# Weight sums of the block products tied to their place in the VectorE order

## The chip, the cores and the metric

The kernel runs on one core of a Trainium2 chip. The metric is the device time in microseconds (us) of one execution of the whole program. Engines are named as the profile names them: PE is TensorE (matmuls), PEld its weight loads, DVE is VectorE, ACT is ScalarE, POOL is GpSimd and SP is SyncE, which here issues nearly all DMAs. Each engine works through its instructions in one fixed order and waits at the head of that order for whatever the next instruction needs.

## The reference

A decoder trunk of two layers on x of 512 tokens by 1024 features. A layer is a half-step SwiGLU feed-forward, a gated token mixing of three attention branches, and a second half-step SwiGLU. The change touches only the two feed-forwards of each layer:

```python
def _swiglu(t, w_gate, w_up, w_down):
    return (jax.nn.silu(t @ w_gate) * (t @ w_up)) @ w_down

for l in range(L):
    f = _swiglu(_rmsnorm(h, ffn1_pre_g[l]), ffn1_w_gate[l], ffn1_w_up[l], ffn1_w_down[l])
    h = h + 0.5 * _rmsnorm(f, ffn1_post_g[l])
    ...   # mixing: stick-breaking, forgetting and memory attention, gated and merged
    f = _swiglu(_rmsnorm(h, ffn2_pre_g[l]), ffn2_w_gate[l], ffn2_w_up[l], ffn2_w_down[l])
    h = h + 0.5 * _rmsnorm(f, ffn2_post_g[l])
```

D_MODEL is 1024 and D_FF is 2816, that is 22 tiles of 128 hidden rows. Everything is float32.

## The kernel before

**Precision.** Every float32 operand of a matmul is split into a high part in a shorter format and a low part that holds the rest. ScalarE makes the high part of a weight tile (line 182, `wh`), and VectorE then the low part from the raw tile and the high one (line 183, `wl`). TensorE does three matmuls for each product (lines 205 to 207): high by high, high by low, low by high.

**The four feed-forwards.** They are called a and c: 0a and 0c in layer 0, 1a and 1c in layer 1 (the letter stands in each name; the order rows below cut the layer's number). Of the 22 hidden tiles the first sixteen, two chunks of eight (ci = 0 and 1), are computed with seven block products in place of eight, as in Strassen's and Winograd's schemes; the remaining six tiles (16 to 21) are plain matmuls ("plain pairs"), and are put between the block products. For each chunk there is a gate group and an up group of seven products (`token_products`, called token-major since the tokens stand on the output's partitions), in this text G0, U0, G1 and U1. Then comes one down group for both chunks (`products`), in which the two chunks take turns.

**A weight unit.** A product n (0, 2, 1, 3, 4, 5, 6 in this order) consists of two units, k = 0 and k = 2, each of two weight tiles of 128 x 512. The unit `gc_1_2_0` is the gate of feed-forward c, chunk 1, product 2, k = 0; `da_1_1_0` is of the down group of a, chunk 1, product 1. `fetch` brings a unit's raw block by one DMA of 512 KB (line 297, on the SP queue, when a slot of the ring `raw` or `o` has come free). For n = 2, 3, 5 and 6, `load` first makes a **weight sum** on VectorE (line 327): a difference of the raw block and a kept block (`tg`, `tu` or `bt`), which takes the place of one of the two. Then ScalarE casts (line 182), and VectorE makes the low part (line 183). High and low parts live in rings of four buffers, so a unit can be split only when TensorE is done with the unit four places back. TensorE works twelve matmuls on a unit. `BlockUnit` (line 270 on) holds all this. There are 192 weight sums in the program: 128 in the token-major groups and 64 in the down groups.

**What else is on VectorE and ScalarE in these groups.** In the gate and up groups: sums of the activations (lines 700 to 725, tiles x00, x11 and others, with their splits `uh` and `ul`), evictions of the products from PSUM (lines 775 to 786), and `turn`, which transposes a finished block of hidden activations: ScalarE copies it apart (line 800, tiles `th`), SP issues a DMA that transposes (line 801, `tr`), and ScalarE copies the result back into the hidden rows `hr` (line 804). In the down group: the first factors (lines 838 to 846, tiles `as`) and their splits `ah` and `al`.

**What sets the order.** Units are loaded ahead of their use by a queue object `Q`, in Python's order of tracing. The tile framework's scheduler then sets the order of each engine and may move an instruction ahead of others that it doesn't depend on. `tc.keep_in_program_order(ins)` adds an edge without a semaphore: `ins` stays behind the instruction that was traced last before it on the same engine. In the kernel before, a weight sum gets that edge only while `Q.pinned` is set, which is a short stretch outside these groups.

## Time and profile before

| what | us |
| --- | --- |
| median of three runs | 2383.31 |
| lowest and highest run | 2377.81 and 2385.16 |
| the profiled execution | 2377.93 |
| its span in the profile | 2376.2 |
| TensorE busy in the span | 2347.3 |
| VectorE busy | 1800.1 |
| ScalarE busy | 1511.8 |

The granted clock of TensorE is 0.996 of full speed over the span. The profiled execution is one near the fast end of the three runs. A row of the timeline gives the start, the length, the engine, line and operation with output and inputs, and in brackets the idle time of that engine just before and what ended it. Rows of the profile cut the numbers of a unit (`wl_dc` for all down units of c); which unit a row is follows from its place in the order.

### The profile page before, as it was taken

How to read it: one execution, taken by the hardware profiler on the slowest of the kernel's cores; microseconds unless marked ns; L12 is line 12 of the kernel's file. 1: busy time of each engine (PE TensorE's matmuls, PEld its weight loads, DVE VectorE, ACT ScalarE, POOL GpSimd, SP SyncE). 2: the span in 40 equal slices, each digit the busy share in tenths (PEclk: the TensorE clock that was granted, in tenths of full speed). 3: DMA queues.
4: the chain of work that ended last, by engine and by line, in shares of the span. 5: the costliest groups of instructions: out<-in, count | busy, mean ns of one | idle time of the engine just before them, and what ended most of it. 6: DMA issues, size and time to landing. Idle time of an engine off the chain costs nothing.

```text
span 2376.2 us, 31130 instructions
## 1 busy us (share of the span) xinstructions
PE 2347.3 (99%) x11719; PEld 1986.0 (84%) x11719; DVE 1800.1 (76%) x2358; ACT 1511.8 (64%) x2305; POOL 75.4 (3%) x134
## 2 busy tenths in 40 slices
PE   9999999999999999999999999999999999999998
PEld 7787889888888888878888878899888888888787
DVE  8876877677777688868788768766767777887785
ACT  6776465576766556774556765646777665567744
POOL 0000000000111000000000000000000100000000
PEclk9999999999999999999999999999999999999999
DMA  5666454223323555664646664542323235566743
GB/s 204 185 177 199 154 190 142 80 83 88 89 74 104 192 189 160 186 186 146 226 127 198 205 171 147 194 129 72 94 76 98 72 117 188 174 185 175 214 144 142
DMA packets 299754, 354.98 MB, mean 149 GB/s; under 512 B 78266, under 2 KB 192978, under 8 KB 299604
## 3 DMA queue, kind: packets, MB, share of 16 engines
q1 hardware_dynamic: 299508, 352.97, 48.5%
q8 instruction: 92, 1.51, 0.3%
q14 instruction: 58, 0.48, 0.1%
q0 software_dynamic: 96, 0.03, 0.0%
HBM read 319.39 MB, written 16.78 MB: 141 GB/s over the span
## 4 chain that ended last, share of the span: by engine, by line
PE 89%; DMA 3%; DVE 3%; ACT 2%; issue 1%; SPq 0%; POOL 0%; DVEq 0%; ACTq 0%
PE pg L206 4%; PE pg L207 4%; PE pg L205 4%; PE pda L206 3%; PE pdc L206 3%; PE pda L207 3%; PE pda L205 3%; PE pdc L207 2%; PE pdc L205 2%; PE pb L206 2%; PE pb L207 2%; PE pb L205 2%; PE pwo L206 1%; PE pq L206 1%; PE pq L205 1%
## 5 line engine op out<-in xcount | busy, mean ns | idle before, releaser
L205 PE MATMUL pg<-us_a,wh_wg 128*128 128x512 f32 x384 | 151.0, 393 | 0.0
L206 PE MATMUL pg<-us_a,wh_wg 128*128 128x512 f32 x384 | 149.8, 390 | 0.0
L207 PE MATMUL pg<-us_a,wl_wg 128*128 128x512 f32 x384 | 149.8, 390 | 0.0
L206 PE MATMUL pda<-wl_da,aha 128*128 128x512 f32 x224 | 89.0, 398 | 6.6 <-DVE wl_da L183 6.6
L206 PE MATMUL pdc<-wl_dc,ahc 128*128 128x512 f32 x224 | 88.7, 396 | 6.1 <-DVE wl_dc L183 6.1
L183 DVE TENSOR_TENSOR wl_da<-raw_da,wh_da 128x1024 fp32r<-128x1024 f32 x50 | 60.8, 1223 | 37.4 <-ACT wh_da L182 37.3
L205 PE MATMUL pda<-wh_da,aha 128*128 128x512 f32 x224 | 88.2, 397 | 0.8 <-ACT wh_da L182 0.5
L207 PE MATMUL pda<-wh_da,ala 128*128 128x512 f32 x224 | 88.4, 395 | 0.0
L183 DVE TENSOR_TENSOR wl_dc<-raw_dc,wh_dc 128x1024 fp32r<-128x1024 f32 x50 | 60.9, 1222 | 35.8 <-ACT wh_dc L182 35.8
L207 PE MATMUL pdc<-wh_dc,alc 128*128 128x512 f32 x224 | 87.9, 393 | 0.0
L205 PE MATMUL pdc<-wh_dc,ahc 128*128 128x512 f32 x224 | 87.4, 393 | 0.4 <-ACT wh_dc L182 0.4
L207 PEld LDWEIGHTS pg<-us_a,wl_wg 128*128 128x128 f32 x384 | 72.1, 188 | 15.2
L205 PEld LDWEIGHTS pg<-us_a,wh_wg 128*128 128x128 f32 x384 | 72.1, 188 | 14.1
L206 PEld LDWEIGHTS pg<-us_a,wh_wg 128*128 128x128 f32 x384 | 72.2, 188 | 14.1
L182 ACT CAST wh_da<-raw_da 128x1024 fp32r<-128x1024 f32 x50 | 52.1, 1049 | 41.1 <-PE pda L207 11.1
L186 DVE SCALAR_TENSOR_TENSOR wl_wg<-raw_wg,wh_wg 128x1024 fp32r<-128x1024 f32 x48 | 58.4, 1221 | 23.0 <-ACT wh_wg L185 23.0
L182 ACT CAST wh_dc<-raw_dc 128x1024 fp32r<-128x1024 f32 x50 | 52.1, 1047 | 35.3 <-DMA raw_dc<-in_ffn_w_down_dram 11.5
L200 DVE SCALAR_TENSOR_TENSOR ga<-pg,bgate,ga 128x512 f32<-128x512 f32 x48 | 35.9, 747 | 48.7 <-ACT ga L199 48.7
L182 ACT CAST wh_uc<-raw_uc 128x1024 fp32r<-128x1024 f32 x44 | 46.4, 1054 | 37.6 <-PE pwc0g L207 8.6
L185 ACT ACTIVATE wh_wg<-raw_wg 128x1024 fp32r<-128x1024 f32 x48 | 50.5, 1057 | 25.5 <-PE pv L1096 11.7
L183 DVE TENSOR_TENSOR wl_uc<-raw_uc,wh_uc 128x1024 fp32r<-128x1024 f32 x44 | 53.7, 1220 | 16.7 <-ACT wh_uc L182 16.6
L182 ACT CAST wh_ua<-raw_ua 128x1024 fp32r<-128x1024 f32 x44 | 46.2, 1052 | 28.7 <-PE pga L206 7.2
(647 smaller groups left out, 8057.2 us busy)
## 6 DMA issues: line engine op xcount, KB each, us to landing
raw_da<-in_ffn_w_down_dram SPq DMA_DIRECT2D x66, 512.0 KB, 4.9
raw_dc<-in_ffn_w_down_dram SPq DMA_DIRECT2D x66, 512.0 KB, 3.8
raw_ga<-in_ffn_w_gate_dram SPq DMA_DIRECT2D x52, 512.0 KB, 4.7
raw_ua<-in_ffn_w_up_dram SPq DMA_DIRECT2D x52, 512.0 KB, 4.6
raw_gc<-in_ffn_w_gate_dram SPq DMA_DIRECT2D x52, 512.0 KB, 4.1
raw_uc<-in_ffn_w_up_dram SPq DMA_DIRECT2D x52, 512.0 KB, 4.2
raw_wg<-in_w_gate_dram SPq DMA_DIRECT2D x48, 512.0 KB, 3.5
raw_wo<-in_w_out_dram SPq DMA_DIRECT2D x24, 512.0 KB, 3.6
```

The lines of the kernel that those rows point to most:

```text
L182: both = [nc.scalar.copy(h_ap, src)]
L183: make = lambda: nc.vector.tensor_tensor(l_ap, src, h_ap.bitcast(F32), ALU.subtract)
L185: both = [nc.scalar.activation(h_ap, src, AF.Copy, scale=scale)]
L186: make = lambda: nc.vector.scalar_tensor_tensor(l_ap, src, scale, h_ap.bitcast(F32), ALU.mult, ALU.subtract)
L200: nc.vector.scalar_tensor_tensor(t, z, minus, t, ALU.max, ALU.add)
L205: nc.tensor.matmul(pt, lh, rh, start=start, stop=False, skip_group_check=free)
L206: nc.tensor.matmul(pt, lh, rl, start=False, stop=False, skip_group_check=free)
L207: nc.tensor.matmul(pt, ll, rh, start=False, stop=stop, skip_group_check=free)
```

## The change

Units get a flag `behind`, which is set for all units of the token-major and the down groups. Where it is set, the weight sum gets the edge of `keep_in_program_order`: it stays behind the VectorE instruction that was traced last before it, which is mostly the low split (line 183) of the unit loaded before. No instruction is added, and none is taken away. In the changed file lines after 816 are shifted by 2, and after 894 by 4.

```diff
--- before.py
+++ after.py
@@ -284,7 +284,7 @@
         def __init__(self, n, src, rows, k0, nk, ncol, keep, name, place="raw"):
             super().__init__(src, k0, nk, 0, ncol, name)
             self.n, self.rows, self.keep, self.fetched, self.place = n, rows, keep, False, place
-            self.heir = None
+            self.heir, self.behind = None, False
 
         def inherits(self, un):
             un.heir, self.place = self, None
@@ -325,7 +325,7 @@
                 src = raw if self.n == 5 else t
                 a, b = (t, raw) if self.n in (2, 5) else (raw, t)
                 ins = nc.vector.tensor_tensor(src, a, b, ALU.subtract)
-                if Q.pinned:
+                if Q.pinned or self.behind:
                     tc.keep_in_program_order(ins)
             self.split_from(src)
             self.loaded()
@@ -815,6 +815,8 @@
             for n in ORDER:
                 uns = [BlockUnit(n, w, ND // 2, k, 2, S, keep, f"{nm}_{n}_{k}", n in (2, 4) or next(places))
                        for k in range(0, ND // 2, 2)]
+                for un in uns:
+                    un.behind = True
                 if n in (2, 4):
                     for un, of in zip(uns, had[n - 2 + (n == 4)]):
                         un.inherits(of)
@@ -893,6 +895,8 @@
                 w = wd[l, ci * FC * P:(ci + 1) * FC * P]
                 uns = [BlockUnit(n, w, FC // 2, k, 2, S, keep[ci], f"d{name}_{ci}_{n}_{k}", ("raw", "o")[k // 2])
                        for k in range(0, FC // 2, 2)]
+                for un in uns:
+                    un.behind = True
                 if n == 4:
                     for un, of in zip(uns, had[ci, 3]):
                         un.inherits(of)
```

What moves, at three places of feed-forward 0c (the other three have the same rows there). First VectorE in the down group, where the second product starts (`dc_0_1` and `dc_1_1`), with the sums `btc_0_0` and `btc_0_2` for the units `dc_0_2_0` and `dc_0_2_2`. Before:

```order
L183 TENSOR_TENSOR wl_dc_0_1_0_9333<-raw_dc_0_1_0_9294,wh_dc_0_1_0_9332 128x1024
L838 TENSOR_TENSOR asc_0_2_9490<-hrc_0_8495,hrc_1_8454 128x1024
L183 TENSOR_TENSOR wl_dc_0_1_2_9341<-raw_dc_0_1_2_9296,wh_dc_0_1_2_9340 128x1024
L327 TENSOR_TENSOR btc_0_0_9336<-btc_0_0_9336,raw_dc_0_2_0_9338 128x1024
L327 TENSOR_TENSOR btc_0_2_9344<-btc_0_2_9344,raw_dc_0_2_2_9346 128x1024
L183 TENSOR_TENSOR wl_dc_1_1_0_9391<-raw_dc_1_1_0_9302,wh_dc_1_1_0_9390 128x1024
L183 TENSOR_TENSOR alc_0_2_9489<-asc_0_2_9490,ahc_0_2_9488 128x1024
L838 TENSOR_TENSOR asc_1_2_9560<-hrc_2_9097,hrc_3_9056 128x1024
L183 TENSOR_TENSOR wl_dc_1_1_2_9397<-raw_dc_1_1_2_9304,wh_dc_1_1_2_9396 128x1024
```

After, from the same row on:

```order
L183 TENSOR_TENSOR wl_dc_0_1_0_9333<-raw_dc_0_1_0_9294,wh_dc_0_1_0_9332 128x1024
L183 TENSOR_TENSOR wl_dc_0_1_2_9341<-raw_dc_0_1_2_9296,wh_dc_0_1_2_9340 128x1024
L183 TENSOR_TENSOR wl_dc_1_1_0_9391<-raw_dc_1_1_0_9302,wh_dc_1_1_0_9390 128x1024
L183 TENSOR_TENSOR alc_0_2_9489<-asc_0_2_9490,ahc_0_2_9488 128x1024
L840 TENSOR_TENSOR asc_1_2_9560<-hrc_2_9097,hrc_3_9056 128x1024
L183 TENSOR_TENSOR wl_dc_1_1_2_9397<-raw_dc_1_1_2_9304,wh_dc_1_1_2_9396 128x1024
L327 TENSOR_TENSOR btc_0_0_9336<-btc_0_0_9336,raw_dc_0_2_0_9338 128x1024
L842 TENSOR_TENSOR asc_0_2_9490<-asc_0_2_9490,hrc_0_8495 128x1024
L183 TENSOR_TENSOR wl_dc_0_2_0_9428<-btc_0_0_9336,wh_dc_0_2_0_9427 128x1024
L327 TENSOR_TENSOR btc_0_2_9344<-btc_0_2_9344,raw_dc_0_2_2_9346 128x1024
```

The two sums stood ahead of the splits of `dc_1_1_0` and `dc_1_1_2`. Now both stand behind them, and each stands two rows ahead of the split of its own unit.

Second, VectorE at the end of U1, where the last up units `uc_1_6_0` and `uc_1_6_2` alternate with the first down units. Here `tuc_1_0` and `tuc_1_2` are the sums for these two units, and lines 777 and 784 are evictions of products. Before (the sum `tuc_1_0` stands six rows further up):

```order
L327 TENSOR_TENSOR tuc_1_2_8825<-raw_uc_1_6_2_9105,tuc_1_2_8825 128x1024
L183 TENSOR_TENSOR wl_dc_0_0_2_9155<-raw_dc_0_0_2_8991,wh_dc_0_0_2_9154 128x1024
L784 TENSOR_TENSOR sc_1_01_8858<-hrc_3_9056,sc_1_01_8858 128x1024
L183 TENSOR_TENSOR wl_uc_1_6_0_9187<-tuc_1_0_8823,wh_uc_1_6_0_9186 128x1024
L777 TENSOR_TENSOR hrc_3_9056<-hrc_3_9056,pwc0u_0_0_8955 128x2x256
L777 TENSOR_TENSOR hrc_3_9056<-hrc_3_9056,pwc0u_0_1_8956 128x2x256
L183 TENSOR_TENSOR alc_1_0_9253<-hrc_2_9097,ahc_1_0_9252 128x1024
L183 TENSOR_TENSOR wl_uc_1_6_2_9192<-tuc_1_2_8825,wh_uc_1_6_2_9191 128x1024
```

After:

```order
L183 TENSOR_TENSOR alc_1_0_9253<-hrc_2_9097,ahc_1_0_9252 128x1024
L183 TENSOR_TENSOR wl_dc_0_0_2_9155<-raw_dc_0_0_2_8991,wh_dc_0_0_2_9154 128x1024
L784 TENSOR_TENSOR sc_1_01_8858<-hrc_3_9056,sc_1_01_8858 128x1024
L327 TENSOR_TENSOR tuc_1_0_8823<-raw_uc_1_6_0_9063,tuc_1_0_8823 128x1024
L777 TENSOR_TENSOR hrc_3_9056<-hrc_3_9056,pwc0u_0_0_8955 128x2x256
L777 TENSOR_TENSOR hrc_3_9056<-hrc_3_9056,pwc0u_0_1_8956 128x2x256
L183 TENSOR_TENSOR alc_0_1_9349<-hrc_1_8454,ahc_0_1_9348 128x1024
L183 TENSOR_TENSOR wl_uc_1_6_0_9187<-tuc_1_0_8823,wh_uc_1_6_0_9186 128x1024
L327 TENSOR_TENSOR tuc_1_2_8825<-raw_uc_1_6_2_9105,tuc_1_2_8825 128x1024
L784 TENSOR_TENSOR sc_1_11_8770<-hrc_3_9056,sc_1_11_8770 128x1024
L183 TENSOR_TENSOR wl_uc_1_6_2_9192<-tuc_1_2_8825,wh_uc_1_6_2_9191 128x1024
```

The sums have come to stand between the splits: `tuc_1_0` behind the split of `dc_0_0_2` and the eviction at line 784, `tuc_1_2` behind the split of `uc_1_6_0`. The split `alc_1_0` has moved ahead of the split of `dc_0_0_2`, and `alc_0_1` ahead of that of `uc_1_6_0`.

Third, ScalarE in G1, around the casts of `uc_0_6_2`, `gc_1_2_0` and `gc_1_2_2`, with the copies to (line 800) and from (line 804) the transposing DMAs. Before:

```order
L804 COPY hrc_0_8495<-trc0u_1_8529 128x2x4x128
L182 CAST wh_uc_0_6_2_8591<-tuc_0_2_8221 128x1024
L800 COPY thc0u_4_1_8618<-sc_0_01_8258 128x1024
L804 COPY hrc_1_8454<-trc0u_4_0_8613 128x2x4x128
L182 CAST wh_gc_1_2_0_8637<-tgc_1_0_8505 128x1024
L800 COPY thc0u_5_0_8668<-sc_0_11_8163 128x1024
L182 CAST wh_gc_1_2_2_8644<-tgc_1_2_8507 128x1024
L800 COPY thc0u_5_1_8671<-sc_0_11_8163 128x1024
L804 COPY hrc_1_8454<-trc0u_4_1_8614 128x2x4x128
```

After:

```order
L800 COPY thc0u_4_1_8618<-sc_0_01_8258 128x1024
L182 CAST wh_uc_0_6_0_8586<-tuc_0_0_8219 128x1024
L804 COPY hrc_1_8454<-trc0u_4_0_8613 128x2x4x128
L804 COPY hrc_1_8454<-trc0u_4_1_8614 128x2x4x128
L182 CAST wh_uc_0_6_2_8591<-tuc_0_2_8221 128x1024
L800 COPY thc0u_5_0_8668<-sc_0_11_8163 128x1024
L800 COPY thc0u_5_1_8671<-sc_0_11_8163 128x1024
L182 CAST wh_gc_1_2_0_8637<-tgc_1_0_8505 128x1024
L804 COPY hrc_1_8454<-trc0u_5_8666 128x2x4x128
L182 CAST wh_gc_1_2_2_8644<-tgc_1_2_8507 128x1024
```

The cast of `uc_0_6_2` now stands behind the copies back of both halves of product 4's transposition, and that of `gc_1_2_2` behind the copy back of the first half of product 5's.

## Prediction

> **What bounds the kernel now.** I read the page first, for the shares and for what TensorE waits for:
>
> ```profile
> span 2376.2 us, 31130 instructions
> PE 2347.3 (99%) x11719; PEld 1986.0 (84%) x11719; DVE 1800.1 (76%) x2358; ACT 1511.8 (64%) x2305; POOL 75.4 (3%) x134
> ```
>
> and then TensorE's waits (total, times, longest):
>
> ```profile
> PE pda L206 <- DVE wl_da L183: 6.6, 2, 4.3
> PE pdc L206 <- DVE wl_dc L183: 6.1, 2, 4.4
> ```
>
> TensorE is the bound, with 29 us of idle in the span. A change of the other engines' order can win only what TensorE idles or runs slowly, and 12.7 us of its waits are for low splits of down units. The timeline of VectorE, and that of TensorE below it, show the place in 0c:
>
> ```profile
> 1048.54 1.23 DVE L183 TENSOR_TENSOR wl_dc<-raw_dc,wh_dc 128x1024 fp32r<-128x1024 f32 x1 [0.31 <-ACT wh_dc L182]
> 1052.86 1.23 DVE L327 TENSOR_TENSOR btc<-btc,raw_dc 128x1024 f32<-128x1024 f32 x1 [3.10 <-DMA raw_dc<-in_ffn_w_down_dram]
> 1056.37 1.23 DVE L327 TENSOR_TENSOR btc<-btc,raw_dc 128x1024 f32<-128x1024 f32 x1 [2.28 <-DMA raw_dc<-in_ffn_w_down_dram]
> 1057.51 1.22 DVE L183 TENSOR_TENSOR wl_dc<-raw_dc,wh_dc 128x1024 fp32r<-128x1024 f32 x1
> 1058.64 1.22 DVE L183 TENSOR_TENSOR alc<-asc,ahc 128x1024 fp32r<-128x1024 f32 x1
> 1059.78 1.22 DVE L838 TENSOR_TENSOR asc<-hrc,hrc 128x1024 f32<-128x1024 f32 x1
> 1060.91 1.22 DVE L183 TENSOR_TENSOR wl_dc<-raw_dc,wh_dc 128x1024 fp32r<-128x1024 f32 x1
> ```
>
> ```profile
> 1053.87 0.50 PE L205 MATMUL pdc<-wh_dc,ahc 128*128 128x512 f32 x1 [0.44 <-ACT wh_dc L182]
> 1058.78 0.79 PE L206 MATMUL pdc<-wl_dc,ahc 128*128 128x512 f32 x1 [4.41 <-DVE wl_dc L183]
> 1059.38 0.63 PE L207 MATMUL pdc<-wh_dc,alc 128*128 128x512 f32 x1
> 1059.80 0.63 PE L205 MATMUL pdc<-wh_dc,ahc 128*128 128x512 f32 x1
> ```
>
> The split of `dc_1_1_0` at 1057.51 stands behind two sums (`btc_0_0`, `btc_0_2`) that wait for DMAs of units used later. TensorE has nothing else and sits for 4.41 us, and then runs a matmul each 0.43 us instead of each 0.23. The same place comes once in each feed-forward. I took the size from windows of 25 us around the four places, with an undisturbed one (1000 to 1025) as the measure; x is the count of matmuls, and the column ahead of the DMA share is the clock:
>
> ```profile
> core 0: us, PE busy (x) PEld busy (x) DVE busy (x) ACT busy (x) POOL busy (x), PEclk, DMA share, GB/s
> 205.00:230.00 25.00, 22.69 (x93) 18.31 (x92) 16.59 (x15) 16.37 (x19) 3.27 (x5) 0.93 0.66 183
> 1000.00:1025.00 25.00, 25.00 (x112) 20.71 (x111) 17.54 (x17) 16.20 (x20) 0.00 (x0) 1.00 0.69 176
> 1050.00:1075.00 25.00, 20.15 (x80) 15.89 (x78) 15.20 (x13) 11.47 (x13) 0.00 (x0) 0.86 0.46 150
> 1390.00:1415.00 25.00, 19.92 (x77) 15.59 (x77) 16.21 (x14) 12.96 (x15) 1.41 (x2) 0.86 0.49 144
> 2225.00:2250.00 25.00, 23.32 (x102) 18.70 (x101) 17.54 (x16) 16.91 (x20) 0.00 (x0) 1.00 0.65 175
> ```
>
> Against 112 matmuls the four lack 19, 32, 35 and 10: 96 matmuls of 25/112 = 0.223 us, **21.4 us**. That is the whole of what the change can win at this place, idle time and low clock together.
>
> **The change part by part.** *The down place.* Both sums go behind the splits of `dc_1_1_0` and `dc_1_1_2`. Nothing else moves ahead of `dc_1_1_0`, so its split starts when its cast is done. ScalarE's timeline has that cast:
>
> ```profile
> 1049.88 2.55 ACT L804 COPY hrc<-trc0u 128x1024 uint16<-128x1024 uint16 x2
> ...
> 1052.78 1.98 ACT L182 CAST wh_dc<-raw_dc 128x1024 fp32r<-128x1024 f32 x2
> ```
>
> The row of two casts begins at 1052.78; half of it is one cast, which ends at about 1053.8. The split then lasts to 1055.0 instead of 1058.73, and TensorE, ready at about 1054.1 (1053.87 and one step of 0.23), still waits 0.9 us. Then come `alc_0_2`, `asc_1_2` and the split of `dc_1_1_2`, three steps of 1.137 us (1057.51 to 1058.64 is one): the last ends at 1058.5, while TensorE, with eleven matmuls of 0.227 us left from 1055.0 and one of the next unit, wants it at 1057.7. That is 0.8 more, so 1.7 us stay. I take 1.4 for the mean of four places, since 0a and 1c lost less before (19 and 10 matmuls against 32 and 35): **5.5 us stay**; the ends are 0 (casts earlier) and 4 x 4.4 = 17.6 (the wait is handed on whole). The sums delayed here are wanted late: the plain units of tiles 18 and 19 stand between, and the blocks they wait for landed at 1052.86 and 1056.37, ahead of 1058.5. The slots that the sums free come free later by about what TensorE comes earlier, so I cost the later fetches at nothing; if that cover fails, the next sums wait as `btc_0_2` did, 2.28 us each.
>
> *The end of U1.* Here the sums `tuc_1_0` and `tuc_1_2` were done early, and now stand between the splits. The rows are of VectorE, ScalarE and TensorE in 0c, and of VectorE and TensorE for the same split in 0a:
>
> ```profile
> 1026.08 1.22 DVE L183 TENSOR_TENSOR wl_dc<-raw_dc,wh_dc 128x1024 fp32r<-128x1024 f32 x1 [3.38 <-ACT wh_dc L182]
> 1027.22 1.22 DVE L784 TENSOR_TENSOR sc<-hrc,sc 128x1024 f32<-128x1024 f32 x1
> 1028.36 1.22 DVE L183 TENSOR_TENSOR wl_uc<-tuc,wh_uc 128x1024 fp32r<-128x1024 f32 x1
> 1029.49 1.28 DVE L777 TENSOR_TENSOR hrc<-hrc,pwc0u 128x512 f32<-128x512 f32 x2
> 1023.79 1.35 ACT L804 COPY hrc<-trc0u 128x1024 uint16<-128x1024 uint16 x1 [4.67 <-DMA trc0u<-thc0u]
> 1031.64 0.39 PE L206 MATMUL pwc0u<-wl_uc,us_b 128*128 128x512 f32 x1
> 1034.36 0.39 PE L206 MATMUL pwc0u<-wl_uc,us_b 128*128 128x512 f32 x1
> ...
> 189.60 1.22 DVE L183 TENSOR_TENSOR wl_ua<-tua,wh_ua 128x1024 fp32r<-128x1024 f32 x1
> 194.36 0.39 PE L206 MATMUL pwa0u<-wl_ua,us_x 128*128 128x512 f32 x1
> ```
>
> The ScalarE copy at 1023.79 came only when its transposing DMA had landed, and all else here follows it. Laid out by the new order with 1.137 us steps: `alc_1_0` starts at 1026.1, the split of `dc_0_0_2` at 1027.2, line 784 at 1028.3, the sum at 1029.5, line 777 (1.2) at 1030.6, `alc_0_1` at 1031.8, the split of `uc_1_6_0` at 1033.0. It ends at 1034.2, where TensorE wants it at 1031.64: 2.5 us late. In the new order of SP the transposing DMA goes out one fetch earlier, which can take back up to all of it. The second split ends three steps later, at 1037.6, against 1034.36 + 2.5: 0.7. So 3.2 us in 0c. In 0a the same split led by 3.5 us (189.60 + 1.22 to 194.36) where in 0c it led by 2.1 (1028.36 + 1.22 to 1031.64), so 1.8 are left there, and I take 0a for 1a and 1c too: 3.2 + 3 x 1.8 = 8.6 at most, 0 at least. I take **5 us**, a little above the middle, since the waits at the transposing DMAs are long.
>
> *G1.* The casts of `uc_0_6_2` and `gc_1_2_2` now stand on ScalarE behind copies back that wait for transposing DMAs:
>
> ```profile
> 953.61 1.22 DVE L784 TENSOR_TENSOR sc<-hrc,sc 128x1024 f32<-128x1024 f32 x1
> 960.38 1.36 ACT L804 COPY hrc<-trc0u 128x1024 uint16<-128x1024 uint16 x1 [1.98 <-DMA trc0u<-thc0u]
> 963.64 0.39 PE L206 MATMUL pwc0g<-wl_gc,uhc 128*128 128x512 f32 x1
> ```
>
> `sc_0_11` is ready at 954.8. Behind it the new order puts two copies out (1.0 each), a cast, the DMA, the copy back (1.36), the cast of `gc_1_2_2` (1.0) and its split (1.2), for a use at 963.64 (`uc_0_6_2` has a chain of the same kind one product earlier). Without the DMA this is 6.6 us, to 961.4, so a DMA that adds under 2.2 us to the chain costs nothing, and each us above shows on TensorE. This price isn't in the trace, as no cast stood so; the ends are 0 and 2.5 a feed-forward (the nearest waits for transposing DMAs are 1.98 here and 4.67 above, against 2.2 in hand). I take 0.75, nearer to the first row, which is of this place: **3 us**.
>
> *Sum, cast and split in a row.* Where a sum directly precedes its own split, VectorE idles for the cast:
>
> ```profile
> 237.80 1.22 DVE L183 TENSOR_TENSOR wl_da<-bta,wh_da 128x1024 fp32r<-128x1024 f32 x1 [1.19 <-ACT wh_da L182]
> ```
>
> By the two orders such neighbours grow from none to four in most U0, G1 and U1 groups: 4 x 1.19 = 4.8 us of 60 us of TensorE work. VectorE is 76% busy, so it has 14 us of idle there, and the splits lead by several us: nothing. In G0 the splits of product 3 move back three steps. In 0a that one ended at 54.55 and is used at 57.63:
>
> ```profile
> 53.33 1.22 DVE L183 TENSOR_TENSOR wl_ga<-tga,wh_ga 128x1024 fp32r<-128x1024 f32 x1
> 57.63 0.39 PE L206 MATMUL pwa0g<-wl_ga,uha 128*128 128x512 f32 x1
> ```
>
> 3.4 us later it is 0.4 us late: **0.5 us**.
>
> *Sum:* -21.4 + 5.5 + 5 + 3 + 0.5 = **-7.4 us**. The profiled execution took 2377.93 (1.7 us outside its span) and becomes 2370.5. The median of the runs lies 5.4 above it, so on that scale I expect 2375.9, say 2376.
>
> *A rule that bears on the stalls.* In 0a the wait was 6.6 - 4.3 = 2.3 us and the clock of its window fell to 0.93; in 1c it was 6.1 - 4.4 = 1.7 us and the clock stayed at 1.00. So a new wait of over about 2 us is followed by a slow stretch. [...]
>
> **The rivals.** *Slower: casts held behind the copies back.* If the transposing DMAs land no earlier, or later, the casts behind them on ScalarE hold splits and TensorE both at U1's end and in G1: 8.6 and 4 x 2.5 = 10 us, and a slow stretch of about 2 us (nine matmuls at 0.43 instead of 0.23) once in each feed-forward, 26.6 instead of 8: 2376 + 18.6, about 2395. By 0.3% (7.1 us, about what a measurement here tells from no change) the kernel is slower once the loss at these two places passes 8 + 7.4 + 7.1 = 22.5, or 5.6 a feed-forward. For it: the 4.67 us wait at 1023.79. Against: the lead in 0a, and the transposing DMAs' place ahead of fetches. *Same: the wait is handed on.* ScalarE's copies back at 1049.88 hold the cast of `dc_1_1_0`; if they come later by what U1 lost, 3 us and a slow stretch of 1 stay at each place, 16 instead of 5.5: 2387. *Full gain.* Nothing new shows: -21.4 + 5.5 = -16, 2367. *The change does nothing* (the edges tie the sums to instructions that leave them where they were): against it stands the order, in which the pair at the down place has moved.
>
> **How the numbers follow.** Forecast 0.37 (of it 0.23 faster by over 0.3%, 0.14 within); full gain 0.18, faster; handed on 0.12, within; slower rival 0.31, slower; nothing 0.02. So faster 0.41, within 0.28, slower 0.31. The range goes from the full 21.4 (2362) to the slower rival (2395).
>
> **What would show it.** Right: no L327 row with a wait for a DMA ahead of the split of `dc_1_1_0`, TensorE's waits for `wl_da` and `wl_dc` at L183 down from 12.7 to under 6, windows around the four places with 100 matmuls or more and clock near 1.00; new waits of TensorE for `wl_uc` and `wl_ua` of 1 to 2 us at U1's end, and of under 1 us for `wl_gc` and `wl_ga` in G1. Wrong: waits for `wl` of up or gate units that sum to over 15 us, a clock under 0.95 at U1's end, or copies at L804 with waits for a DMA as long as before at more places.

## The result, and the profile after

The change made the kernel slower: 2392.57 us median (2389.18 to 2397.53) against 2382.55 (2377.81 to 2385.16) of the kernel before, each from seven runs. The ratio is 1.0045, with an interval of 1.0031 to 1.0059. I had forecast 2376 and thus the wrong direction; the range (2362 to 2395) holds the median.

The page of the kernel after, whose profiled execution took 2392.57:

```profile
span 2390.9 us, 31083 instructions
PE 2354.0 (98%) x11719; PEld 1984.5 (83%) x11719; DVE 1801.0 (75%) x2358; ACT 1509.8 (63%) x2305; POOL 73.4 (3%) x134
```

The count of matmuls, casts and sums is the same and VectorE and ScalarE are busy as long as before. TensorE's busy time has grown by 6.7 us with the same 11719 matmuls, and its idle time from 29 to 37 us. The granted clock over the span is no lower than before (0.997, before 0.996), so the longer busy time is not more slow matmuls: a wait costs more than its idle time shows (0.90 and 1.39 us of delay for 0.74 and 1.12 of idle at the end of U1 in 0c, below). TensorE's waits after (total, times, longest), some of those in the feed-forwards:

```profile
PE pda L205 <- ACT wh_da L182: 3.1, 3, 1.4
...
PE pdc L206 <- DVE wl_dc L183: 2.5, 4, 0.8
PE pda L206 <- DVE wl_da L183: 2.3, 3, 0.8
...
PE pwa1u L206 <- DVE wl_ua L183: 1.6, 2, 1.1
PE pwa0u L206 <- DVE wl_ua L183: 1.6, 2, 1.1
PE pdc L205 <- ACT wh_dc L182: 1.6, 1, 1.6
```

The two waits of over 4 us are gone: down units at L183 went from 12.7 us to 4.8. In their place stand many short ones, none over 1.6: for the casts of down units (L182), for up units in both layers, and for gate units.

The windows of 25 us around the four down places, moved along with the place (in 0a, 0c, 1a and 1c; x is the count of matmuls, the column ahead of the DMA share the clock):

```profile
210.60:235.60 25.00, 23.66 (x102) 18.76 (x101) 17.39 (x16) 18.17 (x22) 2.27 (x5) 1.00 0.64 180
1060.70:1085.70 25.00, 24.32 (x107) 19.55 (x106) 19.16 (x17) 12.92 (x16) 0.00 (x0) 1.00 0.64 219
1399.40:1424.40 25.00, 23.13 (x94) 18.42 (x93) 16.25 (x14) 13.62 (x16) 1.18 (x3) 0.93 0.56 190
2237.30:2262.30 25.00, 22.66 (x98) 17.86 (x97) 17.09 (x15) 17.87 (x21) 0.00 (x0) 1.00 0.65 178
```

Against 112 they lack 10, 5, 18 and 14 matmuls, 47 in place of 96: 47 x 0.223 = 10.5 us stay, where I had 5.5.

**Where the time went, place by place.** Windows alone can't add up the rest, since everything behind the first loss is shifted. So I matched each matmul, by the names of its operands, with the same matmul in the profile of before, and took how much the difference of their start times grew between the first and the last matmul of each stretch. These are differences between single profiled executions, in us, summed over the four feed-forwards; the last column is the whole difference of the two profiled times. "Tails" are the plain pairs behind the down group's last block products.

| kernel | G0 | G1 | end of U1 | down place | rest of down | tails | start and mixing | sum |
| --- | --- | --- | --- | --- | --- | --- | --- | --- |
| forecast | 0.5 | 3 | 5 | -15.9 | 0 | 0 | 0 | -7.4 |
| after | 1.7 | 4.6 | 10.5 | -11.4 | 0 | 8.3 | 1.0 | 14.7 |
| after, another execution | 2.6 | 4.2 | 10.8 | -5.7 | 0 | 5.7 | 0.1 | 17.7 |
| before, another execution | 0.1 | 0.5 | 0 | 1.2 | 0 | 0.2 | 1.4 | 3.3 |

The profile of before lies 4.6 us under its median and that of after on its own, so 14.7 between these profiles is 10.0 between the medians.

**The end of U1**, in 0c after. VectorE (from 1032.42), then TensorE:

```profile
1032.42 1.23 DVE L183 TENSOR_TENSOR alc<-hrc,ahc 128x1024 fp32r<-128x1024 f32 x1 [3.12 <-ACT ahc L182]
1033.57 1.22 DVE L183 TENSOR_TENSOR wl_dc<-raw_dc,wh_dc 128x1024 fp32r<-128x1024 f32 x1
...
1035.84 1.22 DVE L327 TENSOR_TENSOR tuc<-raw_uc,tuc 128x1024 f32<-128x1024 f32 x1
...
1039.30 1.22 DVE L183 TENSOR_TENSOR wl_uc<-tuc,wh_uc 128x1024 fp32r<-128x1024 f32 x1
```

```profile
1037.82 0.39 PE L207 MATMUL pdc<-wh_dc,alc 128*128 128x512 f32 x1
1038.95 0.51 PE L205 MATMUL pwc0u<-wh_uc,us_b 128*128 128x512 f32 x1 [0.74 <-ACT wh_uc L182]
1040.57 0.50 PE L206 MATMUL pwc0u<-wl_uc,us_b 128*128 128x512 f32 x1 [1.12 <-DVE wl_uc L183]
...
1041.73 0.63 PE L207 MATMUL pwc0u<-wh_uc,us_b 128*128 128x512 f32 x1
1042.16 0.63 PE L205 MATMUL pwc0u<-wh_uc,us_b 128*128 128x512 f32 x1
```

VectorE runs in the order and in the steps of 1.14 us that I had laid out, from the wait at 1032.42 through the sum at 1035.84 to the split of `uc_1_6_0`, which ends at 1040.5. TensorE starts that unit's first matmul 0.90 us late (1038.95 against 1037.82 + 0.23) and the second 1.39 late, 2.3 together, and then goes through a stretch of 0.43 us for each matmul. The clock in the windows around it, of 0c and of 0a:

```profile
1036.00:1046.00 10.00, 8.14 (x28) 6.04 (x27) 9.97 (x10) 9.45 (x10) 0.00 (x0) 0.83 0.46 105
192.00:202.00 10.00, 8.88 (x38) 6.66 (x36) 9.97 (x11) 7.09 (x7) 0.00 (x0) 1.00 0.69 191
```

So 0c lost 4.1 us, and 0a, 1a and 1c 2.3, 2.2 and 2.0, without a slow stretch (the clock is 1.00 from 192 to 202 in 0a, from 1370 to 1390 in 1a and from 2220 to 2240 in 1c). The wait that leads this chain is ScalarE's for the transposing DMA:

```profile
1029.95 1.36 ACT L804 COPY hrc<-trc0u 128x1024 uint16<-128x1024 uint16 x1 [3.29 <-DMA trc0u<-thc0u]
```

In the kernel before this row stood at 1023.79, with 4.67 us of wait. TensorE's first low matmul of `uc_1_6_0` went from 1031.64 to 1040.57, of which 2.3 is the new wait, so TensorE was 6.6 us later by then, and the DMA landed 6.2 later: 0.4 us of the help that I thought could be 2.5. The DMA itself did get shorter, as I had thought (7.4 us from its issue at 1016.34 before, 5.6 from 1024.36 after), but it was issued 8.0 us later, 1.4 more than TensorE.

**The tails**, which I had not looked at, in 1a. In this stretch the matched matmuls start 5.5 us later than in the kernel before. The last of the four sums of product 6 (in the kernel after that for `da_1_6_2`), the last cast of such a sum, the first cast of a raw block of the plain pairs, and the cast of the block that is fetched last (the first of two in its row), before:

```profile
1481.57 1.22 DVE L327 TENSOR_TENSOR bta<-raw_da,bta 128x1024 f32<-128x1024 f32 x1
1489.28 1.05 ACT L182 CAST wh_da<-bta 128x1024 fp32r<-128x1024 f32 x1 [1.66 <-PE pua L206]
1492.69 1.04 ACT L182 CAST wh_da<-raw_da 128x1024 fp32r<-128x1024 f32 x1
...
1508.87 2.00 ACT L182 CAST wh_da<-raw_da 128x1024 fp32r<-128x1024 f32 x2 [0.32 <-DMA raw_da<-in_ffn_w_down_dram]
```

and after, with TensorE's waits:

```profile
1494.83 1.22 DVE L327 TENSOR_TENSOR bta<-raw_da,bta 128x1024 f32<-128x1024 f32 x1
1496.13 1.05 ACT L182 CAST wh_da<-bta 128x1024 fp32r<-128x1024 f32 x1 [2.84 <-DVE bta L327]
1499.21 1.05 ACT L182 CAST wh_da<-raw_da 128x1024 fp32r<-128x1024 f32 x1
...
1517.23 1.99 ACT L182 CAST wh_da<-raw_da 128x1024 fp32r<-128x1024 f32 x2 [2.48 <-DMA raw_da<-in_ffn_w_down_dram]
1518.33 0.49 PE L205 MATMUL pda<-wh_da,hida 128*128 128x512 f32 x1 [1.42 <-ACT wh_da L182]
1519.59 0.80 PE L206 MATMUL pda<-wl_da,hida 128*128 128x512 f32 x1 [0.76 <-DVE wl_da L183]
```

The last sum comes 13.3 us later, 7.8 of it against TensorE. In the kernel before, it had ended 6.5 us ahead of the last cast of a sum, and that cast waited for TensorE. Now the cast waits 2.84 us for the sum, and the first raw cast, which stands behind it on ScalarE, is 6.5 us later than before, 1.0 of it against TensorE. From there the loss grows through the fetches. Six of the nine raw blocks of the plain pairs share two slots, so such a fetch goes out when the split of the block two places ahead is done. The last of these fetches goes out at 1510.69 in place of 1504.43, 0.8 later against TensorE, and takes 6.5 us to land in place of 4.4 (why the landing takes longer I did not take apart). Its cast is 8.4 us later than before, 2.9 against TensorE, which waits 1.42 and 0.76 us and then goes through a slow stretch (the clock is 0.83 from 1515 to 1525). By the matched matmuls this tail lost 3.8 us.

The slots that the sums themselves free are not the way here. In both kernels two of the plain pairs' fetches wait for a sum of product 6, and after the change they go out late, but the casts of the blocks that they bring (the first is the row at 1499.21) wait for no DMA.

### The profile page after: what moved, and what is told of

Read it like the earlier page. It is cut to its first block, busy times and chain, and to the rows that moved or that the text cites. A ratio compares the mean times of both kernels' runs of the same rounds, so it can differ in the third digit from the quotient of the medians.

```text
span 2390.9 us, 31083 instructions
## 1 busy us (share of the span) xinstructions
PE 2354.0 (98%) x11719; PEld 1984.5 (83%) x11719; DVE 1801.0 (75%) x2358; ACT 1509.8 (63%) x2305; POOL 73.4 (3%) x134
## 4 chain that ended last, share of the span: by engine, by line
PE 78%; DVE 6%; DMA 6%; ACT 6%; issue 3%; ACTq 0%; SPq 0%; POOL 0%; DVEq 0%
PE pg L206 4%; PE pg L205 4%; PE pg L207 4%; PE pda L206 2%; PE pda L207 2%; PE pda L205 2%; PE pdc L206 2%; PE pdc L207 2%; PE pdc L205 2%; PE pb L207 1%; PE pb L206 1%; PE pb L205 1%; PE pq L206 1%; PE pq L205 1%; PE pk L207 1%
## 5 line engine op out<-in xcount | busy, mean ns | idle before, releaser
L183 DVE TENSOR_TENSOR wl_da<-raw_da,wh_da 128x1024 fp32r<-128x1024 f32 x50 | 60.8, 1222 | 46.9 <-ACT wh_da L182 46.4
L183 DVE TENSOR_TENSOR wl_dc<-raw_dc,wh_dc 128x1024 fp32r<-128x1024 f32 x50 | 60.9, 1222 | 43.0 <-ACT wh_dc L182 42.6
L207 PEld LDWEIGHTS pg<-us_a,wl_wg 128*128 128x128 f32 x384 | 72.1, 188 | 15.2
L206 PEld LDWEIGHTS pg<-us_a,wh_wg 128*128 128x128 f32 x384 | 72.2, 188 | 14.1
L205 PEld LDWEIGHTS pg<-us_a,wh_wg 128*128 128x128 f32 x384 | 72.2, 188 | 14.1
L182 ACT CAST wh_da<-raw_da 128x1024 fp32r<-128x1024 f32 x50 | 51.9, 1050 | 38.6 <-DMA raw_da<-in_ffn_w_down_dram 14.3
L182 ACT CAST wh_dc<-raw_dc 128x1024 fp32r<-128x1024 f32 x50 | 52.0, 1048 | 35.3 <-DVE raw_dc L327 13.4
L183 DVE TENSOR_TENSOR wl_ua<-raw_ua,wh_ua 128x1024 fp32r<-128x1024 f32 x44 | 53.5, 1220 | 13.5 <-ACT wh_ua L182 13.4
L183 DVE TENSOR_TENSOR wl_uc<-raw_uc,wh_uc 128x1024 fp32r<-128x1024 f32 x44 | 53.5, 1221 | 13.3 <-ACT wh_uc L182 13.1
L183 DVE TENSOR_TENSOR wl_gc<-raw_gc,wh_gc 128x1024 fp32r<-128x1024 f32 x40 | 48.3, 1221 | 13.9 <-ACT wh_gc L182 13.4
```

The source lines that it names most:

```text
L182: both = [nc.scalar.copy(h_ap, src)]
L183: make = lambda: nc.vector.tensor_tensor(l_ap, src, h_ap.bitcast(F32), ALU.subtract)
L205: nc.tensor.matmul(pt, lh, rh, start=start, stop=False, skip_group_check=free)
L206: nc.tensor.matmul(pt, lh, rl, start=False, stop=False, skip_group_check=free)
L207: nc.tensor.matmul(pt, ll, rh, start=False, stop=stop, skip_group_check=free)
```

## The experiments

Theories, by the letters that the expectations use. **A**: each sum gains or loses where it stands, and the parts add up. **B**: the loss is idle time of VectorE, spread over all groups. **C**: at the down place the wait is handed on to ScalarE's cast. **D**: the loss at U1's end comes with the transposing DMAs, from the whole group. **E**: the waits for gate units come from sums of the up groups. **F**: the sum of product 5 in U1 makes ScalarE's chain late. **G**: the down place varies from run to run. **H**: a late eviction of product 1 in U1 (line 779) does it.

All kernels change only where the flag is set: the first of the two places is in `token_products` (line 819), the second in `products` (line 899). Nothing is left out of the computation in any of them. Their places, measured in the same way:

| sums kept in place | ratio (interval) | G0 | G1 | end of U1 | down place | rest of down | tails | sum |
| --- | --- | --- | --- | --- | --- | --- | --- | --- |
| all down | 0.9963 (0.9950 to 0.9975) | 0 | -1.8 | 0 | -17.1 | 0.1 | 6.0 | -12.9 |
| all token-major | 1.0061 (1.0049 to 1.0073) | 2.6 | 4.1 | 10.9 | -5.9 | 0 | -0.1 | 9.9 |
| down, product 2 | 0.9932 (0.9921 to 0.9944) | 0.1 | -1.1 | 0 | -17.5 | 0.1 | -0.4 | -17.5 |
| all but down product 6 | 1.0029 (1.0018 to 1.0040) | 2.6 | 4.1 | 9.1 | -14.1 | 1.8 | 0.3 | 2.3 |
| all but U1 product 6 | 1.0000 (0.9991 to 1.0008) | 2.6 | 3.7 | 0 | -11.1 | 0 | 6.0 | 2.7 |
| all but every product 6 | 0.9989 (0.9980 to 0.9998) | 1.8 | 4.8 | 0 | -9.3 | 0.9 | -0.3 | -1.0 |
| U1 product 6 | 1.0033 (1.0021 to 1.0044) | 0 | 2.5 | 6.7 | 3.1 | 0 | 1.0 | 13.6 |
| gates | 1.0042 (1.0029 to 1.0056) | 1.7 | 6.9 | 0 | 4.5 | 0 | -1.1 | 12.4 |
| down product 2, U1 product 5 | 0.9914 (0.9901 to 0.9928) | 0 | -0.2 | 0 | -16.2 | 0 | 0.6 | -14.5 |
| all but every product 6, U1 product 5 | 0.9985 (0.9976 to 0.9994) | 2.6 | 5.4 | 0.6 | -11.2 | 1.9 | -1.2 | -1.6 |
| down product 2, U1 product 3 | 0.9924 (0.9911 to 0.9936) | 0 | -1.0 | 0 | -15.2 | 0.1 | 0.5 | -16.9 |
| all but every product 6, U1 | 0.9949 (0.9935 to 0.9963) | 2.6 | 3.6 | 0 | -14.7 | 1.5 | 0 | -8.0 |

What is missing from a sum is "start and mixing", -1.7 to 1.5 in each. The sums compare one profile with the first profile of before; the ratios compare with runs of before taken beside those of the kernel, so the two need not agree. A place is known only roughly: G1 reads -1.8 to 2.5 in kernels where no gate sum is kept, and the down place -5.9 to 4.5 where no down sum is kept.

**The two halves of the change.** Down sums alone:

```diff
@@ token_products, line 819
-                    un.behind = True
+                    un.behind = False
```

> Only the down groups' units have the flag; the gate and up groups are as before. Theory A (every group of sums costs or wins where it stands, and the parts add): no new waits in the gate groups and at the end of U1; at the four down places about 11 us won, at the plain tail of the down group (the units after the last product, whose fetches start late) about 8 us lost; together 2 to 4 us faster than before, so not to be told from no change. Theory B (the loss is one thread, the idle of VectorE between sum, cast and split everywhere): a third of the sums has the flag, so a third of the loss of the whole change and the full gain, 6 to 10 us faster, with the tail's loss under 3 us.

and token-major sums alone:

```diff
@@ products, line 899
-                    un.behind = True
+                    un.behind = False
```

> Only the gate and up groups' units have the flag; the down groups are as before. Theory A: G0 loses about 2 us, G1 5, the end of U1 10; the four down places keep the waits of before and the plain tails lose nothing: 15 to 18 us slower than before. Theory B: the loss is spread over G1, U0 and U1 alike and no single place of a feed-forward loses over 1.5 us.

Measured: 2365.88 against 2376.21 (ratio 0.9963) and 2389.09 (1.0061). I had expected 2 to 4 us faster and 15 to 18 slower; both came out better, by the down place. The win at the down place comes from the down sums, and all of it: -17.1 us, a little more than I had forecast. The losses in G0, G1 and at U1's end come from the token-major sums, in the sizes of the whole change (2.6, 4.1 and 10.9). The 6.0 us in the tails come from the down sums themselves. The halves do not seem to add: by their medians -10.3 and +12.9 make +2.6, where the whole change is +10.0. The totals alone leave that open, since by the ratios -0.37% and +0.61% make +0.24% against +0.45%, and each has an interval of some 0.13% to either side. In the places the missing part is the down place, which wins 17.1 alone and 11.4 or 5.7 together with the token-major sums, so A holds for the other places and not for this one. With token-major sums alone the place still has its long waits, if shorter than in the first profile of before (8.8 us in place of 12.7):

```profile
PE pdc L206 <- DVE wl_dc L183: 5.0, 2, 2.7
PE pda L206 <- DVE wl_da L183: 3.8, 2, 2.1
```

**Which down sums win, and which lose.** Only product 2 of the down group (16 sums):

```diff
@@ token_products, line 819
-                    un.behind = True
+                    un.behind = False
@@ products, line 899
-                    un.behind = True
+                    un.behind = n == 2
```

> Only the sums of product 2 of the down groups have the flag, sixteen in all; the pair ahead of the split of the second chunk's product 1 is among them. Theory A: the four places win 11 to 16 us, nothing else changes, the plain tails least of all: 11 to 16 us faster than before. Theory C (the wait at the place is handed on to ScalarE's cast behind the copies back, whatever stands on VectorE): at most 5 us faster.

and all but product 6 of the down group:

```diff
@@ products, line 899
-                    un.behind = True
+                    un.behind = n != 6
```

> The whole change, but the sums of product 6 of the down groups are free as before. Theory A, with the cause of the tail's loss in these sums (they free the slots that the plain tail's blocks are fetched into): the four plain tails lose under 2 us together instead of 8, so 6 to 8 us faster than the whole change and about 2 to 4 us slower than before. If the tail's loss has another cause (transposing DMAs or other sums ahead of it), it stays at about 8 us, and the time at that of the whole change.

The first gave 2360.38 (2358.1 to 2361.59) against 2376.21. Its windows at the four places:

```profile
204.60:229.60 25.00, 25.00 (x110) 20.11 (x109) 18.82 (x17) 17.48 (x20) 3.27 (x5) 1.00 0.73 189
1046.90:1071.90 25.00, 24.17 (x105) 19.19 (x104) 18.99 (x17) 13.19 (x16) 0.00 (x0) 1.00 0.67 230
1380.70:1405.70 25.00, 23.86 (x103) 18.92 (x102) 18.04 (x16) 14.07 (x16) 0.71 (x1) 1.00 0.67 224
2209.30:2234.30 25.00, 25.00 (x111) 20.23 (x110) 18.62 (x16) 16.56 (x19) 0.00 (x0) 1.00 0.65 183
```

They lack 2, 7, 9 and 1 matmuls, 19 x 0.223 = 4.2 us, against my 5.5 that stay. So the term for the down place was right for the edit that it describes: 16 of the 192 sums make it, and the other down sums add nothing there that shows (17.1 with all of them).

The second kernel settles which sums cost the tails: 0.3 in place of 8.3. In 1a the last sum and the last cast of a sum are back where they were before the change, and the cast waits for TensorE again:

```profile
1480.93 1.22 DVE L327 TENSOR_TENSOR bta<-raw_da,bta 128x1024 f32<-128x1024 f32 x1
1488.51 1.05 ACT L182 CAST wh_da<-bta 128x1024 fp32r<-128x1024 f32 x1 [1.66 <-PE pua L206]
```

The kernel as a whole came out 0.29% slower than before, about 7 us where I had expected 2 to 4. In the four kernels that leave only product 6 of the down sums free, the rest of the down group loses 0.9 to 1.9 us, which it does in no other; I did not follow this.

**Which sums lose at U1's end.** All but the eight sums of product 6 in U1; all but every product 6; and those eight sums alone:

```diff
@@ token_products, line 819
-                    un.behind = True
+                    un.behind = not (up and ci == 1 and n == 6)
```

> The whole change, but the eight sums of product 6 of the second chunk's up groups (two at the end of U1 in each feed-forward) are free. Theory A (they alone make the loss at the end of U1, and that loss hides part of the gain at the down place, since the blocks have landed by the time TensorE comes): the end of U1 loses under 1 us in all, the four down places win 16 to 17 us instead of 11; G0, G1 and the plain tails lose as in the whole change: 3 to 7 us faster than the kernel before. Theory D (the loss at the end of U1 comes with the transposing DMAs and copies back that the whole group has moved): 6 us or more stay at the end of U1, and the time is within 2 us of the whole change.

```diff
@@ token_products, line 819
-                    un.behind = True
+                    un.behind = n != 6
@@ products, line 899
-                    un.behind = True
+                    un.behind = n != 6
```

> The whole change without product 6 anywhere (gate, up and down). Theory A: no loss at the end of U1 (under 1 us) and none at the plain tails (under 1 us), the down places win 16 to 17 us, G0 and G1 still lose 4 to 8 us: 8 to 13 us faster than the kernel before.

```diff
@@ token_products, line 819
-                    un.behind = True
+                    un.behind = up and ci == 1 and n == 6
@@ products, line 899
-                    un.behind = True
+                    un.behind = False
```

> Only the eight sums of product 6 of the second chunk's up groups have the flag. Theory A: the end of U1 loses 8 to 10.5 us over the four feed-forwards, the down places lose 4 to 6 us less than before because the blocks that the pair of sums waits for land at the same time and TensorE comes later: 3 to 6 us slower than before. Theory D: under 3 us lost at the end of U1.

Ratios 1.0000, 0.9989 and 1.0033. Without these eight sums the end of U1 loses nothing (0 and 0); alone they lose 6.7 us there (I had expected 8 to 10.5), so the rest of the 10.5 comes only in the company of the other token-major sums. That decides against B and D: the loss at U1's end needs the two sums put between two splits, as I had laid it out, and is not there for the group or its transposing DMAs without them. I had also held it possible that the late end of U1 hides part of the wait at the down place, so that the place wins less once U1 loses nothing. It won 11.1 and 9.3, against 11.4 and 5.7 with the loss, and where the loss stands alone the place lost 3.1: no sign of that. This is also why the first two of these kernels came out at 1.0000 and 0.9989, where I had expected them 3 to 7 and 8 to 13 us faster than the kernel before.

**Where the waits for gate units come from.** Sums of the gate groups alone:

```diff
@@ token_products, line 819
-                    un.behind = True
+                    un.behind = not up
@@ products, line 899
-                    un.behind = True
+                    un.behind = False
```

> Only the gate groups' units have the flag. Theory A: G0 loses 2 to 3 us (in 0a alone), G1 4 to 5 us over the four feed-forwards, the end of U1 and the down places are as before: 6 to 8 us slower than before. Theory E (the gate groups' waits come from the up groups' sums that stand among them): under 3 us slower.

Ratio 1.0042. G1 loses 6.9 us and G0 1.7 by themselves, so E falls. The mechanism in G1 is the one forecast, as the one wait of 0c shows in the kernel after:

```profile
977.44 1.36 ACT L804 COPY hrc<-trc0u 128x1024 uint16<-128x1024 uint16 x1 [2.15 <-DMA trc0u<-thc0u]
978.66 1.04 ACT L182 CAST wh_gc<-tgc 128x1024 fp32r<-128x1024 f32 x1
981.01 0.50 PE L206 MATMUL pwc0g<-wl_gc,uhc 128*128 128x512 f32 x1 [0.77 <-DVE wl_gc L183]
```

A cast stands behind a copy back that waits 2.15 us for its transposing DMA, and TensorE then waits for the split. The unit here is `gc_1_3_2`, one product later than the two that I had priced. In this kernel, whose down groups have the order of before, the down place got worse too:

```profile
PE pdc L206 <- DVE wl_dc L183: 7.3, 2, 4.5
PE pda L206 <- DVE wl_da L183: 7.2, 2, 4.2
```

14.5 us against 12.7.

**Why the down place wins less with the token-major sums.** On record were F and G, and then, as F fell, H. Product 2 of the down group with product 5 of U1, and all but every product 6 and product 5 of U1:

```diff
@@ token_products, line 819
-                    un.behind = True
+                    un.behind = up and ci == 1 and n == 5
@@ products, line 899
-                    un.behind = True
+                    un.behind = n == 2
```

> The sums of product 2 of the down groups, as in the run that had them alone, and besides the eight sums of product 5 of the second chunk's up groups. Theory F (at U1's end a late sum of product 5 makes the chain of copies out, transposing DMAs and copies back about 1.4 us later against TensorE, and that chain ends at the cast that the down place waits for): no wait at the end of U1, and the down places win 10 to 13 us instead of 17.5, so 6 to 10 us faster than the kernel before. Theory G (the down place varies by such amounts from run to run, whatever stands at U1's end): the down places win 16 us or more, 14 to 17 us faster than the kernel before.

```diff
@@ token_products, line 819
-                    un.behind = True
+                    un.behind = not (up and ci == 1 and n in (5, 6))
@@ products, line 899
-                    un.behind = True
+                    un.behind = n != 6
```

> The whole change without products 5 and 6 of the second chunk's up groups and without product 6 of the down groups. If the losses lie where theory A and F put them: G0 loses about 2 us and G1 4, U1's end and the plain tails nothing, the down places win 15 to 18 us: 9 to 12 us faster than the kernel before. If something else of the gate and up groups makes ScalarE's chain late: the down places win 9 to 12 us, 3 to 6 us faster.

F falls twice: product 5 of U1 added to the best kernel costs the place nothing that shows (-16.2 against -17.5; ratio 0.9914), and taken from the other it brings nothing (-11.2, against -9.3 without any product 6 and -14.1 without that of the down groups). Both kernels of the case once more, without an edit, for one profile each:

> The kernel before, unchanged, for a second profile. If the four down places cost what they did in the first (21 us), the comparisons of places stand; if they differ by over 4 us, a place's gain is known only to that.

> The changed kernel, unchanged, for a second profile. The end of U1 loses 9 to 12 us, the plain tails 5 to 9, G0 and G1 together 5 to 8, and the down places win 9 to 14 us against the first profile of before.

The place moved by 1.2 us between two executions of the kernel before and by 5.7 between two of the kernel after (rows of the first table), so differences of a few us there are not to be read from one profile. G thus explains part, though not that all seven profiles of kernels with down sums and most token-major sums win 5.7 to 14.7, while the four with down sums and no token-major ones, or one product of U1, win 15.2 to 17.5. Last, product 3 of U1 with product 2 of the down group, and the change without U1 and without any product 6:

```diff
@@ token_products, line 819
-                    un.behind = True
+                    un.behind = up and ci == 1 and n == 3
@@ products, line 899
-                    un.behind = True
+                    un.behind = n == 2
```

> The sums of product 2 of the down groups, and the eight sums of product 3 of the second chunk's up groups. In VectorE's order of U1 these leave the sums of products 5 and 6 where they were, but put the second half of product 1's eviction (line 779) behind a split that waits for TensorE. Theory H (that late eviction makes the chain of copies out, transposing DMAs and copies back late against TensorE, up to the cast that the down place waits for): the first copy out of product 1 comes 2 to 3.5 us later against TensorE, the down places win 10 to 13 us instead of 17: 7 to 11 us faster than the kernel before. If the lateness comes from elsewhere: the down places win 16 us or more, 14 to 19 us faster.

```diff
@@ token_products, line 819
-                    un.behind = True
+                    un.behind = not (up and ci == 1)
@@ products, line 899
-                    un.behind = True
+                    un.behind = n != 6
```

> The whole change without the second chunk's up groups and without product 6 of the down groups; VectorE's order at U1's end is that of before. Theory H: the down places win 15 to 18 us, G0 loses 2 and G1 4 to 6, the rest nothing: 8 to 12 us faster than the kernel before. If the flags of the gate groups or of U0 make ScalarE's chain late: the down places win 9 to 12 us, 2 to 6 us faster.

Product 3 of U1 costs the place about 2 us (-15.2 against -17.5), no more than two executions can differ by. Without any sum of U1 the place wins 14.7, still 2 to 3 short. So H carries at most 2 us, and of U1's products neither 3 nor 5 alone holds the rest; 2 and 6 were not tried in this company.

What the rows show is where it goes: into theory C. In 1c of the kernel after, ScalarE and then TensorE:

```profile
2243.68 1.36 ACT L804 COPY hrc<-trc1u 128x1024 uint16<-128x1024 uint16 x1 [0.75 <-DMA trc1u<-thc1u]
...
2245.84 2.55 ACT L804 COPY hrc<-trc1u 128x1024 uint16<-128x1024 uint16 x2
...
2248.73 1.99 ACT L182 CAST wh_dc<-raw_dc 128x1024 fp32r<-128x1024 f32 x2
2249.83 0.50 PE L205 MATMUL pdc<-wh_dc,ahc 128*128 128x512 f32 x1 [1.58 <-ACT wh_dc L182]
2251.09 0.50 PE L206 MATMUL pdc<-wl_dc,ahc 128*128 128x512 f32 x1 [0.76 <-DVE wl_dc L183]
```

The cast of `dc_1_1_0` stands behind three copies back, and these behind transposing DMAs. Measured from TensorE's first matmul of `dc_0_1_0`, this cast ends after 4.4 to 6.0 us in the kernel with product 2 alone, after 5.0 to 6.2 in the change without U1, and after 5.2 to 7.2 in the whole change; TensorE wants it at 5.4. The eleven profiles with down sums kept fall in line: the mean of this time over the four places is 5.1 us where 17.5 are won, then 5.2, 5.4, 5.7, 5.8 and 6.0 (17.1, 16.2, 15.2, 14.7 and 14.1), and 6.3 to 7.0 in the five that win 5.7 to 11.4. So the missing gain goes with this cast's lateness. What stays open is which of the token-major sums set how late this chain is. Moving the cast itself ahead of the copies was not tried.

## Why the prediction was wrong

- **The step that failed first** is "so I cost the later fetches at nothing". I had argued it for the sums of product 2 at the down place, where it held (-0.4 in the tails with these alone), and applied it to all down sums. The sums of product 6 cost 8.3 us in the tails in one profile and 5.7 in the other, and leaving them out gives this back (0.3, and -0.3 without any product 6). The fetches do become late, but not by the slots that the sums free: the last sum moved back by 7.8 us against TensorE and had 6.5 us of lead over the last cast of a sum, so that cast, the casts and splits behind it and the fetches that wait for these splits all come late. The lead stands in the profile of before (1481.57 + 1.22 to 1489.28). I had asked for it at the end of U1, and not here.
- **The end of U1** was right in place, order and mechanism, and wrong in size: 10.5 for 5. "Can take back up to all of it" was the error: the transposing DMA landed nearly as much later as TensorE came (6.2 and 6.6 us). Without that credit I had 8.6; the rest is the slow stretch in 0c, which the prediction has, at about 2, only in its slower rival and not in the sum. The three feed-forwards without it lost 2.3, 2.2 and 2.0, against my 1.8.
- **The down place**: mechanism and price were right for the sums that it spoke of (with product 2 alone 17.5 won, my 15.9), and wrong in the company of the others: 10.5 us stay, not 5.5, and some 16 in the second profile (21.4 - 5.7). That is the rival "the wait is handed on", to which I had given 0.12, with its 16 us. I counted it as one case among others; it should have stood in the forecast's own sum, since the cast behind the copies back was in the rows that I showed, ending only 0.3 us ahead of TensorE's need (1053.8 and 1054.1).
- **G1** was 4.6 for 3, by the forecast mechanism, at `gc_1_3_2` as well as at the units named. **G0** was 1.7 to 2.6 for 0.5, and by another cause (last section). **Sum, cast and split in a row** at nothing: the places and the sum column leave no loss for it outside the places named, but no run tested it by itself.
- **The sum.** Forecast -7.4, measured 14.7 between the profiles. The 22 us are 8.3 of tails, 5.5 of U1, 4.5 of the down place, 1.6 of G1, 1.2 of G0 and 1.0 of the rest of the program.
- **The slower rival** gave 26.6 of new losses and 2395; its places lost 15.1 (10.5 and 4.6), above the 8 of the forecast but under the 22.5 from which it would have decided alone. The direction was turned by the tails and the down place, for which it had nothing.
- **The marks** were drawn badly. "Wrong: waits for up or gate units over 15 us" was not reached: they sum to about 11 us, and the waits for down units are under 6, as "right" wanted. Of the other two signs of being wrong, the clock under 0.95 at U1's end was there in 0c (0.83), and copies back waited for their DMA 31 times in place of 23, the longest 3.5 us in place of 4.7. Of the four down places only two had the 100 matmuls that "right" wanted. A wait's row counts idle time only. In 0c at U1's end 0.74 and 1.12 of idle were 0.90 and 1.39 of delay, and 1.8 of slow matmuls followed: 1.9 in the waits, 4.1 in the time.
- **The rule on the clock.** "A new wait of over about 2 us is followed by a slow stretch" was an estimate from two windows of the kernel before (2.3 us of wait with a clock of 0.93, 1.7 with 1.00), and it did not hold: after two waits of 1.9 in sum the clock fell (U1's end in 0c, 0.74 and 1.12, to 0.83; the down place in 1a, 1.11 and 0.76, to 0.93), and after 1.58 and 0.76 in 1c it stayed at 1.00. One pair of waits shows it best, in G0 of 0a (last section): 1.37 and 0.76 us in one execution of the kernel after, 1.38 and 0.76 in the other, and the clock of the window around it was 1.00 and 0.89. In nine profiles with this pair it fell in six; G0 lost 2.6 us in these and 1.7 or 1.8 in the other three. So the length of the waits alone did not decide here whether the clock fell; what did was not shown.

## What to carry over

An edge that ties an instruction to its place holds up more than the next step of its own unit: ask, for each instruction that moves back, how much lead it had over the instruction that waits for it, and what stands in line behind that one on the other engine, down to the fetches. Keep in place only the instructions that block something: the 16 sums of product 2 in the down groups give 2360.38, ratio 0.9932 (0.9921 to 0.9944), and beat both kernels, while the other 176 together cost more than these win (the whole change is at 1.0045); adding product 5 or 3 of U1 (0.9914 and 0.9924) is not told apart from that. And price a wait by the shift of start times, with the slow matmuls behind it, not by the idle time in its row (1.9 us in the rows and 4.1 in the time, at the end of U1 in 0c).

## What the runs showed of the hardware

In G0 of 0a, in the kernel after, ScalarE and the sum on VectorE, and the wait on TensorE:

```profile
60.81 1.28 ACT L1040 ACT_TABLE_LOAD   x1
...
65.83 1.28 ACT L1041 ACT_TABLE_LOAD   x1
67.23 1.03 ACT L182 CAST wh_ga<-raw_ga 128x1024 fp32r<-128x1024 f32 x1
61.96 1.22 DVE L327 TENSOR_TENSOR raw_ga<-tga,raw_ga 128x1024 f32<-128x1024 f32 x1
68.32 0.50 PE L205 MATMUL pwa0g<-wh_ga,uha 128*128 128x512 f32 x1 [1.37 <-ACT wh_ga L182]
```

The sum for `ga_0_5_0` ends at 63.2, but its cast starts only at 67.23: four loads of activation tables of 1.28 us each, one ahead of each of the four instructions of the memory statistics here (lines 1040 and 1041, twice), stand ahead of it on ScalarE. In the kernel before they started at 77.78 and behind, and the cast stood well ahead of them:

```profile
60.33 2.18 ACT L182 CAST wh_ga<-raw_ga 128x1024 fp32r<-128x1024 f32 x2 [0.16 <-PE pwa0g L207]
```

So the 1.7 to 2.6 us of G0, which 0a alone loses, are not the three VectorE steps that I had priced, but a stage whose own work was nowhere near the change. The windows around this wait, of the kernel after and of its other execution, show the clock that makes the difference between 1.7 and 2.6:

```profile
64.00:80.00 16.00, 13.41 (x58) 10.20 (x57) 12.82 (x21) 11.60 (x14) 0.00 (x0) 1.00 0.45 132
64.00:80.00 16.00, 13.87 (x53) 10.72 (x52) 13.17 (x20) 11.56 (x13) 0.00 (x0) 0.89 0.47 136
```
